# Swapping the two halves of a complex state by ScalarE copies instead of second matmuls, with the answers one pair later

## The chip, the cores and the metric

The kernel runs on one core of one Trainium2 chip. The metric is the device time of one execution in microseconds (us); the time before is the median of three runs. A profile is one further execution, taken by the hardware profiler. TensorE multiplies matrices, VectorE, ScalarE and GpSimd work on elements, and SyncE (SP) issues most DMA transfers; each engine carries out its own list of instructions in order and waits on semaphores for the others. In the profile they are PE (and PEld for weight loads), DVE, ACT, POOL and SP.

## The reference

One layer of a decoder trunk on 2048 tokens of width 1024: a norm, one input projection, three mixers side by side (A sliding window attention, B a state space model, C sparse attention), an output projection, and a feed-forward block. The change concerns mixer B, on 32 groups of 16 channels with 64 complex states each:

```python
A = lax.complex(a_re, a_im);  dt = jnp.exp(log_dt)[:, None]
A_bar = jnp.exp(A * dt)
B_bar = ((A_bar - 1.0) / A)[..., None] * Bm
Bu = jnp.einsum('blgp,gnp->blgn', uf, B_bar)
_, states = lax.associative_scan(_scan_combine, (A_bar, Bu), axis=1)   # a_r*a_l, a_r*b_l + b_r
y = jnp.einsum('blgn,gpn->blgp', states, Cm).real + D * uf
z = jax.nn.gelu(y);  ab = z @ glu_w + glu_b
out = ab[..., :W] * jax.nn.sigmoid(ab[..., W:])
```

## The kernel before

The kernel is one program in stages. The first, `phase_front` (line 81), computes the input projection in float32 by splitting each operand into a high and a low part and adding three products (`mm3`, line 74). It runs in two halves of eight row blocks. The 16 row blocks hold every 16th token each. The projection's columns come in five chunks: two u chunks (input of mixer B), then a, b and c; for each chunk `load_w` (line 128) loads eight weight slices, ScalarE converts each to its high part `wh` and VectorE computes the low part `wl`. Two buffers hold raw slices (`wr`), twelve hold `wh` and `wl`, so the last four slices of a chunk have to wait until the chunk before gives its buffers back.

In the second half the state space model is computed beside the products of the a, b and c chunks. `merge` (line 68) puts the two lists of steps together evenly: one half of a product (12 matmuls), one step of `ssm_steps` (line 430), and so on. The scheduler then orders each engine's instructions by its own estimates, so they do not stand in the order of the code. Memory for the state space model (pool `sg`, in `tp`) is that of a pool closed just before; its last user is a one-element copy on VectorE, the gate (line 201), which reads a piece of a `wl` slice. Every first use of the new memory, on whatever engine, waits for the gate.

The 32 groups go in 16 pairs (`GB = 2`). The 2048 tokens of a group lie as 128 chunks of 16. Real parts of the states lie on partitions 0 to 63, imaginary parts on 64 to 127. For pair b:

- `outer` (GpSimd): CA, the output coefficients for 17 powers of the step, three operations.
- `local` (TensorE pk, then kst on VectorE and ScalarE, then a DMA to `dkp`): the response inside a chunk.
- `turned`: `turns` (VectorE, six operations: E, rotation factors), two DMAs that make CS, which is CA with its partition halves exchanged, Wc from `dkp` by DMA, Bp (VectorE), transposes pu and pbt (TensorE), copies U and BT (ScalarE). BT holds 192 columns, the first 64 twice, so that columns 64 to 191 are the exchanged halves.
- `scanned`: pv by eight matmuls, four with the plain halves and four with the exchanged ones (line 522); m, the product with E (line 524), and the sum of its two parts; the scan Q (line 529, one instruction per group); on GpSimd St, Q times both parts of E (line 531).
- `answer`: py from four matmuls per group, two on the inputs (lines 537, 538), one on the first part of St with CA (539) and one on its second part with CS (540); then Gelu into `u_st` and `outer` of a later pair.

The steps of a pair are `scanned(b)` (with `local(b+1)` ahead of it), `turned(b+1)`, `answer(b)`. There is one St, two E, two CS.

Of the kernel before, what the change touches and what calls it, by code (L numbers as in the profile page):

```python
# [7 lines left out]
F32 = mybir.dt.float32  # L8
# [3 lines left out]
ALU = mybir.AluOpType  # L12
# [4 lines left out]
P = 128  # L17
# [63 lines left out]
def phase_front(tc, C, x, norm1_g, w_in, u_st, pd, rh_a, prm, dkp, extra):  # L81

    nc = tc.nc
    with ExitStack() as ctx:
# [96 lines left out]
        S = {}  # L181
        for half in range(2):
            box, hs = {}, []

            def steps_of(ch):
                kind, c0, n = ch
                res = [lambda: (box.update({ch: load_w(half, *ch)}), run(todo), todo.clear())]
                if ch is chunks[0]:
                    res.insert(0, lambda: hs.append(load_h(8 * half)))
                for j in range(8):  # L190
                    if ch is chunks[0] and j < 7:
                        res.append(lambda j=j: hs.append(load_h(8 * half + j + 1)))
                    for part in ((0, 1) if half and kind != "u" else (None,)):
                        res.append(lambda j=j, part=part: product(8 * half + j, hs[j], box[ch], kind, c0, n, part))
                return res
            lists = [steps_of(ch) for ch in chunks]
            with tc.tile_pool(name=f"a_x{half}", bufs=2, **({} if half else {"reuse_waits": "tile"})) as xp:
                box_x[:] = [xp]
                run(lists[0] + (lists[1] + lists[2][:1] if half else []))
                if half:  # L200
                    nc.vector.tensor_copy(xp.tile([1, 1], F32, name="gate", bufs=1), box[chunks[2]][4][1][0:1, 0:1].bitcast(F32))
            if half == 0:
                with tc.tile_pool(name="bv", bufs=1, reuse_waits="tile") as bv:
                    extra(bv, ps_t)
# [222 lines left out]
GB = 2  # L427


def ssm_steps(tc, C, S, u_st, dkp, tp, ps, ps_t):  # L430

    nc = tc.nc
    M = {}
    St = tp.tile([P, GB, 2, P], F32, name="St")
    nc.vector.memset(St[:, :, :, 0:1], 0.0)
# [7 lines left out]

    def turns(b):

        e = M["e", b] = tl([P, GB, 2, P], "E", b, 2)
        u = tl([P, 2, GB, 8, 16], "t2", f"u{b}")
        u1, u2 = u[:, 0], u[:, 1]
        ea = [S["Ea"][:, j, of(b)].unsqueeze(3).broadcast_to([P, GB, 8, 16]) for j in range(2)]
        eb = [S["Eb"][:, j, of(b)].unsqueeze(2).broadcast_to([P, GB, 8, 16]) for j in range(2)]  # L450
        o = [e[:, :, j].rearrange("p g (a b) -> p g a b", b=16) for j in range(2)]
        nc.vector.tensor_tensor(u1, ea[0], eb[0], op=ALU.mult)
        nc.vector.tensor_tensor(u2, ea[1], eb[1], op=ALU.mult)
        nc.vector.tensor_tensor(o[0], u1, u2, op=ALU.subtract)
        nc.vector.tensor_tensor(u1, ea[1], eb[0], op=ALU.mult)
        nc.vector.tensor_tensor(u2, ea[0], eb[1], op=ALU.mult)
        nc.vector.tensor_tensor(o[1], u1, u2, op=ALU.add)

    def outer(b):

        bc = [P, GB, 17, 16]
        CA, t1 = tl(bc, "CA", b, 3), tl(bc, "t1", b)
        ar, ai = (S[n][:, :, of(b)].rearrange("p t g -> p g t").unsqueeze(3).broadcast_to(bc) for n in ("AR", "AI"))
        nc.gpsimd.tensor_tensor(CA, ar, S["C1"][:, of(b)].unsqueeze(2).broadcast_to(bc), op=ALU.mult)
        nc.gpsimd.tensor_tensor(t1, ai, S["C2"][:, of(b)].unsqueeze(2).broadcast_to(bc), op=ALU.mult)
        nc.gpsimd.tensor_tensor(CA, CA, t1, op=ALU.add)
        M["c", b] = CA
# [14 lines left out]
    def turned(b):  # L482

        turns(b)
        CA = M["c", b]
        CS, Wc = tl([P, GB, 16, 16], "CS", b, 2), tl([P, GB, 256], "Wc", b, 2)
        nc.sync.dma_start(CS[0:64], CA[64:P, :, 1:17])
        nc.sync.dma_start(CS[64:P], CA[0:64, :, 1:17])
        for i in range(GB):
            base = dkp[b * GB + i]  # L490
            nc.sync.dma_start(Wc[:, i], bass.AP(base.tensor, base.offset, [[16, 8], [368, 16], [1, 256]]))
        bb = [P, GB, 16, 16]
        Bp, t2 = tl(bb, "Bp", b), tl(bb, "t2", b)
        ar, ai = (S[n][:, 0:16, of(b)].rearrange("p t g -> p g t").unsqueeze(3).broadcast_to(bb) for n in ("AR", "AI"))
        nc.vector.tensor_tensor(Bp, ar, S["Y"][:, of(b)].unsqueeze(2).broadcast_to(bb), op=ALU.mult)
        nc.vector.tensor_tensor(t2, ai, S["W"][:, of(b)].unsqueeze(2).broadcast_to(bb), op=ALU.mult)
        nc.vector.tensor_tensor(Bp, Bp, t2, op=ALU.add)
        pb = ps.tile([P, GB, 2, P], F32, tag="pb", name=f"pbt{b}", bufs=2)
        pu = ps_t.tile([P, GB, 2, P], F32, tag="pt", name=f"pu{b}")
        for i in range(GB):  # L500
            for k in range(2):
                nc.tensor.transpose(pu[:, i, k], u_st[:, b * GB + i, k * P:(k + 1) * P], C["ident"])
        U = tl([P, GB, 2, P], "U", b, 2)
        nc.scalar.copy(U, pu)
        for i in range(GB):
            for k in range(2):
                nc.tensor.transpose(pb[:, i, k], Bp[:, i, 8 * k:8 * k + 8].rearrange("p a b -> p (a b)"), C["ident"])
        BT = tl([P, GB, 2, 192], "BT", b)
        nc.scalar.copy(BT[:, :, :, 0:P], pb)
        nc.scalar.copy(BT[:, :, :, P:192], pb[:, :, :, 0:64])  # L510
        M["b", b] = BT, U, CA, CS, Wc

    def scanned(b):

        if b + 1 < NB:
            local(b + 1)
        BT, U = M["b", b][0:2]
        pv = ps.tile([P, GB, 2, P], F32, tag="pv", name=f"pv{b}")
# [1330 lines left out]
```

## Time and profile before

| | us |
|---|---|
| median of three runs | 2623.99 (2622.14 to 2625.36) |
| the profiled execution | 2620.41 |
| its span, first to last instruction | 2618.6 |

The page gives each engine's busy time over the whole span. What bounds a stage is read from the stage: busy time in a window of the span, and who waited for whom in it. An engine's idle time stands with the instruction that follows it, with the releaser behind the arrow. Matmuls overlap, so a matmul's worth is the distance from start to start, not its duration.

### The profile page before, as it was taken

The page shows a single profiled execution, that of the slowest core. Times are in us where ns is not written, and L with a number is a line of the kernel's source. Part 1 is how long each engine was busy: PE and PEld are TensorE (multiplying, and loading weights), DVE is VectorE, ACT ScalarE, POOL GpSimd, SP SyncE. Part 2 cuts the span into 40 slices and gives each one's busy share as a digit, 9 for nine tenths or more (in the row PEclk, how much of TensorE's full clock was granted, in tenths as well). Part 3 has the DMA queues.
Part 4 walks back from the last instruction along what each step waited for, and adds up shares of the span by engine and source line. Part 5 has one row for each costly group of instructions (what it writes and reads, how often), then busy time and mean ns, then how long its engine had stood idle before and what let it go on. Part 6 is the DMA issues. An engine that isn't in the chain of part 4 may idle for free. (4 is left out here: it accounts for less than half of the span.)

```text
span 2618.6 us, 38744 instructions
## 1 busy us (share of the span) xinstructions
PE 2509.6 (96%) x13096; PEld 2112.8 (81%) x13096; DVE 1784.2 (68%) x3419; ACT 1311.0 (50%) x2726; POOL 1122.8 (43%) x1179
## 2 busy tenths in 40 slices
PE   8999999899899999999989999899999999999999
PEld 7998999677677877777868888688887888888887
DVE  3835774855686667777666555755556888888886
ACT  5344332765575666655545555544444443344442
POOL 2013442221233333323266676656554445454447
PEclk9999999999999999999989999999999999999999
DMA  4342323521222111211266667665546544444435
GB/s 124 91 135 80 87 80 84 157 75 56 70 76 67 62 65 59 83 46 58 66 223 199 179 190 214 202 185 146 153 136 209 180 127 133 132 126 130 124 97 197
DMA packets 398230, 320.99 MB, mean 123 GB/s; under 512 B 52006, under 2 KB 369068, under 8 KB 396208
## 3 DMA queue, kind: packets, MB, share of 16 engines
q1 hardware_dynamic: 361936, 293.36, 37.6%
q10 hardware_dynamic: 36096, 25.17, 2.9%
q8 instruction: 103, 1.69, 0.3%
q14 instruction: 95, 0.78, 0.1%
HBM read 206.26 MB, written 107.99 MB: 120 GB/s over the span
## 5 line engine op out<-in xcount | busy, mean ns | idle before, releaser
L1335 DVE TENSOR_TENSOR v<-vr,v 128x512 fp32r<-128x512 f32 x224 | 240.0, 1080 | 76.8 <-ACT v L1334 76.4
L1334 ACT CAST v<-vr 128x512 fp32r<-128x512 f32 x224 | 139.3, 624 | 304.0 <-DMA vr<-vd 132.9
L1649 PE MATMUL pdc<-dw,v 128*128 128x512 f32 x768 | 186.4, 392 | 5.0 <-ACT dw L1334 3.2
L1649 PE MATMUL pda<-dw,v 128*128 128x512 f32 x768 | 184.5, 389 | 0.0
L1649 PE MATMUL pdb<-dw,v 128*128 128x512 f32 x768 | 184.5, 389 | 0.0
L1649 PEld LDWEIGHTS pdc<-dw,v 128*128 128x128 f32 x768 | 145.1, 189 | 36.4 <-ACT dw L1334 3.6
L1649 PEld LDWEIGHTS pda<-dw,v 128*128 128x128 f32 x768 | 144.2, 188 | 29.9
L1649 PEld LDWEIGHTS pdb<-dw,v 128*128 128x128 f32 x768 | 144.2, 188 | 29.9
L1445 POOL TENSOR_TENSOR fs<-ur,ur 128x512 f32<-128x512 f32 x64 | 96.4, 1507 | 166.2 <-DMA ur<-in_w_up 102.3
L1334 ACT CAST uh<-fs 128x512 fp32r<-128x512 f32 x128 | 78.6, 621 | 148.3 <-PE pub L1474 64.0
L1335 DVE TENSOR_TENSOR ul<-fs,uh 128x512 fp32r<-128x512 f32 x128 | 132.6, 1039 | 22.6 <-ACT uh L1334 22.3
L1335 DVE TENSOR_TENSOR ul<-ur,uh 128x512 fp32r<-128x512 f32 x96 | 101.6, 1062 | 52.4 <-ACT uh L1334 45.9
L76 PE MATMUL pw<-wo_h,mh 128*128 128x512 f32 x256 | 111.0, 434 | 4.9 <-DVE ml L1204 2.7
L857 DVE TENSOR_TENSOR tls<-pps,ths 128x512 fp32r<-128x512 f32 (+1 forms) x144 | 92.8, 658 | 29.9 <-ACT ths L856 22.3
L1490 POOL TENSOR_TENSOR ev<-e,e 128x512 f32<-128x512 f32 x64 | 96.0, 1499 | 36.4 <-ACT e L1487 26.4
L856 ACT CAST ths<-pps 128x512 fp32r<-128x512 f32 (+1 forms) x144 | 79.1, 565 | 57.0 <-PE pps L853 27.2
L77 PE MATMUL pw<-wo_l,mh 128*128 128x512 f32 x256 | 105.9, 414 | 0.0
L1474 PE MATMUL pub<-fl,uh 128*128 128x512 f32 x256 | 102.6, 401 | 3.1 <-DVE fl L1335 3.0
L78 PE MATMUL pw<-wo_h,ml 128*128 128x512 f32 x256 | 105.2, 411 | 0.0
L1474 PE MATMUL pub<-fh,uh 128*128 128x512 f32 x256 | 102.8, 402 | 1.5 <-ACT fh L1334 1.5
L1474 PE MATMUL pua<-fh,uh 128*128 128x512 f32 x256 | 101.3, 396 | 2.2 <-ACT e L1494 2.2
L1474 PE MATMUL pua<-fl,uh 128*128 128x512 f32 x256 | 101.4, 396 | 0.8 <-DVE fl L1335 0.8
(563 smaller groups left out, 7930.6 us busy)
## 6 DMA issues: line engine op xcount, KB each, us to landing
vr<-vd SPq DMA_DIRECT2D x224, 256.0 KB
ur<-in_w_up SPq DMA_DIRECT2D x128, 256.0 KB
vd<-ev SPq DMA_DIRECT2D x128, 256.0 KB
vd<-e ACTq DMA_DIRECT2D x64, 256.0 KB
dr<-in_w_down SPq DMA_DIRECT2D x32, 512.0 KB
x<-in_x SPq DMA_DIRECT2D x16, 512.0 KB
mx<-in_x SPq DMA_DIRECT2D x16, 512.0 KB
x<-mx ACTq DMA_DIRECT2D x16, 512.0 KB
```

The lines of the kernel that those rows point to most:

```text
L76: nc.tensor.matmul(out, sh, mh, start=first, stop=False)
L77: nc.tensor.matmul(out, sh, ml, start=False, stop=False)
L78: nc.tensor.matmul(out, sl, mh, start=False, stop=last)
L856: nc.scalar.copy(th[:, 0:nb], pt[:, 0:nb])
L857: nc.vector.tensor_tensor(tl[:, 0:nb], pt[:, 0:nb], th[:, 0:nb], op=ALU.subtract)
L1334: nc.scalar.copy(dh, src)
L1335: nc.vector.tensor_tensor(dl, src, dh, op=ALU.subtract)
L1445: nc.gpsimd.tensor_tensor(t, x, y, op=op)
L1474: nc.tensor.matmul(bank[b], w[:, k], h[o][:, k], start=first and k == 0 and n == 0, stop=k == HALF - 1 and n == 2, skip_group_check=True)
L1490: nc.gpsimd.tensor_tensor(tile_("v" + o), x, y, op=op)
L1649: nc.tensor.matmul(bank[b, q], x[:, q, j], y[:, j], start=first and j == 0 and n == 0, stop=j == 1 and n == 2, skip_group_check=True)
```

## The change

The exchange of the halves is made by ScalarE. `scanned` computes pv by four matmuls, copies it with its halves exchanged to vs (`swap`, two copies of 64 partitions), multiplies pv and vs each by its part of E and adds. After the scan a second `swap` makes the exchanged Q; GpSimd multiplies both by E in one instruction and subtracts one result from the other in a second. St is then a single state, and the answer needs one state matmul per group; CS with its DMAs and BT's extra columns are gone. There are two St and three E. The steps are now `scanned(b)`, `next_(b)` (`answer(b-1)`, then `local(b+1)`), `turned(b+1)` (which ends with `outer` of the pair after). The gate reads slice 3, not 4.

```diff
-                    nc.vector.tensor_copy(xp.tile([1, 1], F32, name="gate", bufs=1), box[chunks[2]][4][1][0:1, 0:1].bitcast(F32))
+                    nc.vector.tensor_copy(xp.tile([1, 1], F32, name="gate", bufs=1), box[chunks[2]][3][1][0:1, 0:1].bitcast(F32))
...
-    St = tp.tile([P, GB, 2, P], F32, name="St")
+    Ss = [tp.tile([P, GB, P], F32, name=f"St{j}", bufs=1) for j in range(2)]
...
-        e = M["e", b] = tl([P, GB, 2, P], "E", b, 2)
+        e = M["e", b] = tl([P, GB, 2, P], "E", b, 3)
...
-        nc.sync.dma_start(CS[0:64], CA[64:P, :, 1:17])
-        nc.sync.dma_start(CS[64:P], CA[0:64, :, 1:17])
...
-        BT = tl([P, GB, 2, 192], "BT", b)
-        nc.scalar.copy(BT[:, :, :, 0:P], pb)
-        nc.scalar.copy(BT[:, :, :, P:192], pb[:, :, :, 0:64])
+        BT = tl([P, GB, 2, P], "BT", b)
+        nc.scalar.copy(BT, pb)
+        M["b", b] = BT, U, CA, Wc
+        if b + 1 < NB:
+            outer(b + 1)
+
+    def swap(dst, src):
+
+        nc.scalar.copy(dst[0:64], src[64:P])
+        nc.scalar.copy(dst[64:P], src[0:64])
...
-        if b + 1 < NB:
-            local(b + 1)
...
-            for j in range(2):
-                for k in range(2):
-                    nc.tensor.matmul(pv[:, i, j], BT[:, i, k, 64 * j:64 * j + P], U[:, i, k], start=k == 0, stop=k == 1)
-        m, e = tl([P, GB, 2, P], "m", b), M.pop(("e", b))
-        nc.vector.tensor_tensor(m, pv, e, op=ALU.mult)
+            for k in range(2):
+                nc.tensor.matmul(pv[:, i], BT[:, i, k], U[:, i, k], start=k == 0, stop=k == 1)
+        m, e, vs = tl([P, GB, 2, P], "m", b), M.pop(("e", b)), tl([P, GB, P], "vs", b)
+        swap(vs, pv)
+        nc.vector.tensor_tensor(m[:, :, 0], pv, e[:, :, 0], op=ALU.mult)
+        nc.vector.tensor_tensor(m[:, :, 1], vs, e[:, :, 1], op=ALU.mult)
...
-        nc.gpsimd.tensor_tensor(St[:, :, :, 1:P], Q[:, :, 0:n].unsqueeze(2).broadcast_to([P, GB, 2, n]), e[:, :, :, 0:n], op=ALU.mult)
+        swap(Q[:, 1], Q[:, 0])
+        n, t = P - 1, tl([P, 2, GB, P], "t3", b)
+        nc.gpsimd.tensor_tensor(t[:, :, :, 0:n], Q[:, :, :, 0:n], e.rearrange("p g j c -> p j g c")[:, :, :, 0:n], op=ALU.mult)
+        nc.gpsimd.tensor_tensor(Ss[b % 2][:, :, 1:P], t[:, 0, :, 0:n], t[:, 1, :, 0:n], op=ALU.subtract)
...
-            nc.tensor.matmul(py[:, i], St[:, i, 0], CA[:, i, 1:17].rearrange("p a b -> p (a b)"), start=False, stop=False)
-            nc.tensor.matmul(py[:, i], St[:, i, 1], CS[:, i].rearrange("p a b -> p (a b)"), start=False, stop=True)
+            nc.tensor.matmul(py[:, i], Ss[b % 2][:, i], CA[:, i, 1:17].rearrange("p a b -> p (a b)"), start=False, stop=True)
...
-        if b + 2 < NB:
-            outer(b + 2)
...
+    def next_(b):
+        if b:
+            answer(b - 1)
+        if b + 1 < NB:
+            local(b + 1)
```

The order moves with it. On VectorE at the start of the state space model before (wl1_a0_4 is the low part of the fifth slice of the a chunk, t2u0, E0 and Bp0 are temporaries, rotation factors and input coefficients of pair 0):

```order
L144 SCALAR_TENSOR_TENSOR wl1_a0_3_2872<-wr1_a0_3_2869,g1_111,wh1_a0_3_2871 128x384
L144 SCALAR_TENSOR_TENSOR wl1_a0_4_2878<-wr1_a0_4_2875,g1_111,wh1_a0_4_2877 128x384
L144 SCALAR_TENSOR_TENSOR wl1_a0_5_2884<-wr1_a0_5_2881,g1_111,wh1_a0_5_2883 128x384
L201 COPY gate_2899<-wl1_a0_4_2878 1x1
...
L144 SCALAR_TENSOR_TENSOR wl1_a0_6_2890<-wr1_a0_6_2887,g1_111,wh1_a0_6_2889 128x384
L457 TENSOR_TENSOR E0_2955<-t2u0_2956 128x2x128
L144 SCALAR_TENSOR_TENSOR wl1_a0_7_2896<-wr1_a0_7_2893,g1_111,wh1_a0_7_2895 128x384
```

The same place now:

```order
L144 SCALAR_TENSOR_TENSOR wl1_a0_3_2872<-wr1_a0_3_2869,g1_111,wh1_a0_3_2871 128x384
L201 COPY gate_2899<-wl1_a0_3_2872 1x1
...
L496 TENSOR_TENSOR Bp0_2963<-Bp0_2963,t20_2964 128x512
...
L455 TENSOR_TENSOR E1_3058<-t2u1_3059 128x2x128
...
L458 TENSOR_TENSOR E1_3058<-t2u1_3059 128x2x128
L495 TENSOR_TENSOR t21_3070<-k_AI_728,k_W_723 128x512
L144 SCALAR_TENSOR_TENSOR wl1_a0_4_2878<-wr1_a0_4_2875,g1_111,wh1_a0_4_2877 128x384
L144 SCALAR_TENSOR_TENSOR wl1_a0_5_2884<-wr1_a0_5_2881,g1_111,wh1_a0_5_2883 128x384
```

Sixteen state space instructions, all of pair 0's factors and coefficients and most of pair 1's, stand now between the gate and the fifth slice; before, the gate stood behind the sixth.

On TensorE in the middle, around the answer of pair 10 (left out are the products, and the answer's second group, which repeats the first), before:

```order
L475 MATMUL pk11_4246<-CA11_4223,k_Y_722 128x256 x2
L522 MATMUL pv10_4253<-U10_4191,BT10_4197 128x128 x8
L502 MATMUL pu11_4337<-c_ident_60,u_st_83 128x128 x4
L507 MATMUL pbt11_4336<-c_ident_60,Bp11_4331 128x128 x4
...
L537 MATMUL py10_4364<-Wc10_4175,U10_4191 128x256
L538 MATMUL py10_4364<-Wc10_4175,U10_4191 128x128
L539 MATMUL py10_4364<-CA10_4107,St_2905 128x256
L540 MATMUL py10_4364<-CS10_4174,St_2905 128x256
```

and now:

```order
L476 MATMUL pk11_4244<-CA11_4180,k_Y_722 128x256 x2
L501 MATMUL pu11_4316<-c_ident_60,u_st_83 128x128 x4
L506 MATMUL pbt11_4315<-c_ident_60,Bp11_4310 128x128 x4
...
L524 MATMUL pv11_4347<-U11_4321,BT11_4327 128x128 x4
...
L543 MATMUL py10_4385<-Wc10_4158,U10_4172 128x256
L544 MATMUL py10_4385<-Wc10_4158,U10_4172 128x128
L545 MATMUL py10_4385<-CA10_4061,St0_2905 128x256
...
L476 MATMUL pk12_4393<-CA12_4329,k_Y_722 128x256 x2
```

Between the scan of pair 10 and its answer there is now the pv of pair 11; pv has four matmuls, the answer one on the state per group, and pk comes behind the answer.

On ScalarE at the same place (kst, U and BT of a pair, Gelu into u_st, po the result of a product, sq its squares), before:

```order
L479 COPY kst11_4249<-pk11_4246 16x2x240
L504 COPY U11_4342<-pu11_4337 128x512
L509 COPY BT11_4348<-pbt11_4336 128x4x128
L510 COPY BT11_4348<-pbt11_4336 128x4x64
L541 ACTIVATE u_st_83<-py10_4364 128x512
L167 ACTIVATE po8_c_4391<-pm8_c0_4351,r8_2119 128x396
```

and now:

```order
L480 COPY kst11_4247<-pk11_4244 16x2x240
L503 COPY U11_4321<-pu11_4316 128x512
L508 COPY BT11_4327<-pbt11_4315 128x512
L515 COPY vs11_4353<-pv11_4347 64x256
L516 COPY vs11_4353<-pv11_4347 64x256
L167 ACTIVATE po8_c_4379<-pm8_c0_4334,r8_2119 128x396
L169 ACTIVATE sq8_c_4381<-po8_c_4379 128x128
L515 COPY Q11_4359<-Q11_4359 64x256
L516 COPY Q11_4359<-Q11_4359 64x256
L546 ACTIVATE u_st_83<-py10_4385 128x512
L480 COPY kst12_4396<-pk12_4393 16x2x240
```

Four copies of 64 partitions stand now between BT and the Gelu, the last two behind a wait for the scan on VectorE.

## Rows read from the trace of the kernel before

**Rows 1.** Page, part 1: busy us, share of the span, instructions.

```profile
PE 2509.6 (96%) x13096; PEld 2112.8 (81%) x13096; DVE 1784.2 (68%) x3419; ACT 1311.0 (50%) x2726; POOL 1122.8 (43%) x1179
```

**Rows 2.** Busy time by stage: window, length, engines, granted clock, DMA share, GB/s.

```profile
core 0: us, PE busy (x) PEld busy (x) DVE busy (x) ACT busy (x) POOL busy (x), PEclk, DMA share, GB/s
222.00:235.00 13.00, 13.00 (x112) 13.00 (x111) 1.76 (x7) 2.90 (x6) 0.28 (x1) 1.00 0.11 33
235.00:258.00 23.00, 16.80 (x78) 15.23 (x78) 22.19 (x29) 6.65 (x13) 13.84 (x10) 0.78 0.36 92
258.00:458.00 200.00, 196.40 (x1203) 188.49 (x1202) 125.58 (x253) 65.88 (x133) 72.72 (x57) 0.99 0.31 85
```

**Rows 3.** Timeline, TensorE in the middle: start us, duration us, instruction.

```profile
301.22 0.59 PE L540 MATMUL py<-CS,St 128*128 128x256 f32 x2
...
301.65 0.60 PE L537 MATMUL py<-Wc,U 128*128 128x256 f32 x2
...
306.12 1.95 PE L522 MATMUL pv<-U,BT 128*128 128x128 f32 x16
...
307.83 0.42 PE L76 MATMUL pm_a<-wh_a,hh 128*128 128x384 f32 x1
```

**Rows 4.** Groups, 258 to 458 us: count, busy us, mean ns, idle before, releaser.

```profile
L531 POOL TENSOR_TENSOR St<-Q,E 128x508 f32<-128x508 f32 x16 | 21.4, 1335 | 79.2 <-DVE Q L529 50.4 <-DMA wr_b<-in_w_in 9.7 <-PE pm_b L78 6.6
L539 PE MATMUL py<-CA,St 128*128 128x256 f32 x64 | 19.9, 393 | 3.6 <-POOL St L531 3.6
...
L529 DVE TENSOR_TENSOR_SCAN Q<-k_rho,m 128x128 f32<-128x128 f32 x32 | 11.8, 412 | 0.5
...
L453 DVE TENSOR_TENSOR t2u<-k_Ea,k_Eb 128x256 f32<-128x256 f32 x13 | 11.8, 908 | 0.0
...
L452 DVE TENSOR_TENSOR t2u<-k_Ea,k_Eb 128x256 f32<-128x256 f32 x13 | 11.2, 865 | 0.4
...
L524 DVE TENSOR_TENSOR m<-pv,E 128x512 f32<-128x512 f32 x15 | 10.3, 688 | 13.9 <-PE pv L522 13.9
...
L495 DVE TENSOR_TENSOR Bp<-k_AR,k_Y 128x512 f32<-128x512 f32 x14 | 9.6, 684 | 0.0
...
L525 DVE TENSOR_TENSOR m<-m 128x256 f32<-128x256 f32 x16 | 6.8, 425 | 0.5
L454 DVE TENSOR_TENSOR E<-t2u 128x256 f32<-128x256 f32 x14 | 6.0, 426 | 19.0 <-POOL St L531 19.0
...
L510 ACT COPY BT<-pbt 128x256 f32<-128x256 f32 x15 | 5.9, 390 | 0.0
```

**Rows 5.** Timeline, the start: [idle before, releaser].

```profile
233.29 1.15 DVE L144 SCALAR_TENSOR_TENSOR wl_a<-wr_a,g,wh_a 128x384 fp32r<-128x384 f32 x2 [11.11 <-ACT wh_a L143]
234.36 0.13 DVE L201 COPY gate<-wl_a 1x1 f32<-1x1 f32 x1
...
234.72 1.37 POOL L464 TENSOR_TENSOR CA<-k_AR,k_C 128x544 f32<-128x544 f32 x1 [22.98 <-DVE gate L201]
...
236.45 1.12 ACT L143 ACTIVATE wh_a<-wr_a,g 128x384 fp32r<-128x384 f32 x2 [0.84 <-DVE t2u L453]
...
240.48 2.08 PE L475 MATMUL pk<-CA,k_Y 128*128 128x256 f32 x4 [3.27 <-POOL CA L466]
...
249.75 1.11 PE L507 MATMUL pbt<-c_ident,Bp 128*128 128x128 f32 x4 [2.25 <-DVE Bp L497]
...
250.52 0.67 PE L76 MATMUL pm_a<-wh_a,hh 128*128 128x384 f32 x1
```

**Rows 6.** Timeline, VectorE and GpSimd side by side.

```profile
234.97 1.39 DVE L453 TENSOR_TENSOR t2u<-k_Ea,k_Eb 128x256 f32<-128x256 f32 x1
...
247.66 1.49 POOL L465 TENSOR_TENSOR t<-k_AI,k_C 128x544 f32<-128x544 f32 x1
...
249.73 0.42 DVE L452 TENSOR_TENSOR t2u<-k_Ea,k_Eb 128x256 f32<-128x256 f32 x1
```

**Rows 7.** Groups of the whole span, GpSimd on 256 columns.

```profile
L877 POOL TENSOR_TENSOR oa<-ota 128x256 f32<-128x256 f32 x16 | 12.1, 757 | 37.7 <-ACT esa L946 8.7 <-issue 6.4 <-PE cpt L714 6.0
```

**Rows 8.** DMA issues, 258 to 458 us: queue, count, KB each.

```profile
CS<-CA SPq DMA_DIRECT2D x28, 128.0 KB
```

More of the change, by code (lines that the diff above doesn't have):

```diff
@@ L433, in ssm_steps @@
     M = {}
-    St = tp.tile([P, GB, 2, P], F32, name="St")
-    nc.vector.memset(St[:, :, :, 0:1], 0.0)
+    Ss = [tp.tile([P, GB, P], F32, name=f"St{j}", bufs=1) for j in range(2)]
+    for t in Ss:
+        nc.vector.memset(t[:, :, 0:1], 0.0)
     NB = G // GB
@@ L485, in turned @@
         CA = M["c", b]
-        CS, Wc = tl([P, GB, 16, 16], "CS", b, 2), tl([P, GB, 256], "Wc", b, 2)
-        nc.sync.dma_start(CS[0:64], CA[64:P, :, 1:17])
-        nc.sync.dma_start(CS[64:P], CA[0:64, :, 1:17])
+        Wc = tl([P, GB, 256], "Wc", b, 2)
         for i in range(GB):
@@ L507, in turned @@
                 nc.tensor.transpose(pb[:, i, k], Bp[:, i, 8 * k:8 * k + 8].rearrange("p a b -> p (a b)"), C["ident"])
-        BT = tl([P, GB, 2, 192], "BT", b)
-        nc.scalar.copy(BT[:, :, :, 0:P], pb)
-        nc.scalar.copy(BT[:, :, :, P:192], pb[:, :, :, 0:64])
-        M["b", b] = BT, U, CA, CS, Wc
+        BT = tl([P, GB, 2, P], "BT", b)
[6 more added lines that the diff above has]
+        nc.scalar.copy(dst[64:P], src[0:64])
@@ L513, in scanned @@
     def scanned(b):
-        if b + 1 < NB:
-            local(b + 1)
         BT, U = M["b", b][0:2]
-        pv = ps.tile([P, GB, 2, P], F32, tag="pv", name=f"pv{b}")
+        pv = ps.tile([P, GB, P], F32, tag="pv", name=f"pv{b}")
         for i in range(GB):
-            for j in range(2):
-                for k in range(2):
-                    nc.tensor.matmul(pv[:, i, j], BT[:, i, k, 64 * j:64 * j + P], U[:, i, k], start=k == 0, stop=k == 1)
-        m, e = tl([P, GB, 2, P], "m", b), M.pop(("e", b))
@@ L524, in scanned @@
-        nc.vector.tensor_tensor(m, pv, e, op=ALU.mult)
+            for k in range(2):
[4 more added lines that the diff above has]
+        nc.vector.tensor_tensor(m[:, :, 1], vs, e[:, :, 1], op=ALU.mult)
         nc.vector.tensor_tensor(m[:, :, 0], m[:, :, 0], m[:, :, 1], op=ALU.add)
-        Q = tl([P, GB, P], "Q", b)
+        Q = tl([P, 2, GB, P], "Q", b)
@@ L527, in scanned @@
         for i in range(GB):
             g = b * GB + i
-            nc.vector.tensor_tensor_scan(Q[:, i], S["rho16"][:, g:g + 1].to_broadcast([P, P]), m[:, i, 0], 0.0, op0=ALU.mult, op1=ALU.add)
-        n = P - 1
-        nc.gpsimd.tensor_tensor(St[:, :, :, 1:P], Q[:, :, 0:n].unsqueeze(2).broadcast_to([P, GB, 2, n]), e[:, :, :, 0:n], op=ALU.mult)
+            nc.vector.tensor_tensor_scan(Q[:, 0, i], S["rho16"][:, g:g + 1].to_broadcast([P, P]), m[:, i, 0], 0.0, op0=ALU.mult, op1=ALU.add)
+        swap(Q[:, 1], Q[:, 0])
@@ L533, in answer @@
+        n, t = P - 1, tl([P, 2, GB, P], "t3", b)
+        nc.gpsimd.tensor_tensor(t[:, :, :, 0:n], Q[:, :, :, 0:n], e.rearrange("p g j c -> p j g c")[:, :, :, 0:n], op=ALU.mult)
+        nc.gpsimd.tensor_tensor(Ss[b % 2][:, :, 1:P], t[:, 0, :, 0:n], t[:, 1, :, 0:n], op=ALU.subtract)
     def answer(b):
-        _, U, CA, CS, Wc = M.pop(("b", b))
+        _, U, CA, Wc = M.pop(("b", b))
         py = ps.tile([P, GB, 256], F32, tag="py", name=f"py{b}")
@@ L538, in answer @@
             nc.tensor.matmul(py[:, i, P:256], U[:, i, 0], Wc[:, i, 0:P], start=False, stop=False)
-            nc.tensor.matmul(py[:, i], St[:, i, 0], CA[:, i, 1:17].rearrange("p a b -> p (a b)"), start=False, stop=False)
-            nc.tensor.matmul(py[:, i], St[:, i, 1], CS[:, i].rearrange("p a b -> p (a b)"), start=False, stop=True)
+            nc.tensor.matmul(py[:, i], Ss[b % 2][:, i], CA[:, i, 1:17].rearrange("p a b -> p (a b)"), start=False, stop=True)
         nc.scalar.activation(u_st[:, of(b)], py, AF.Gelu_apprx_tanh)
-        if b + 2 < NB:
-            outer(b + 2)
     def first():
         outer(0)
-        outer(1)
         local(0)
+    def next_(b):
[3 more added lines that the diff above has]
+            local(b + 1)
     res = [first, lambda: turned(0)]
     for b in range(NB):
-        res.append(lambda b=b: scanned(b))
+        res += [lambda b=b: scanned(b), lambda b=b: next_(b)]
         if b + 1 < NB:
             res.append(lambda b=b: turned(b + 1))
-        res.append(lambda b=b: answer(b))
-    return res
+    return res + [lambda: answer(NB - 1)]
 def gelu2(nc, t, out, y):
```

## The prediction

> **What bounds the kernel now.** I read the page's busy shares first. TensorE is busy for 96% of the span, VectorE 68%, ScalarE 50%, GpSimd 43% [rows 1]; the reader should take from it only that a stage which gives TensorE less to do can pay everywhere. The stage view comes second, cut at the two ends of the stretch that the diff touches (from the second half's last u product to the end of the front). [...] So there are two places with different limits: a start in which TensorE waits for VectorE and GpSimd, and 200 us in which TensorE sets the pace. The 16 pairs of the state space model share those 200 us, 12.5 us each. Third, the timeline inside one pair, for what a removed matmul is worth [rows 3]. Fourth, the groups of instructions of the stretch, for the other engines' durations and for what TensorE waited for: only the matmul on the state waits, 3.6 us in all, for GpSimd's St [rows 4].
>
> **What goes from TensorE.** Eight pv matmuls of a pair start at 306.12 and the next matmul at 307.83, 1.71 us [rows 3]; four of eight remain, so 0.855 us go per pair, 13.7 us over 16. The second state matmul of a group holds the engine from 301.22 to 301.65, 0.43 us [rows 3]; 32 of them go, 13.8 us. Together 27.5 us, and all of it lies on the engine that sets the pace. The 3.6 us wait for St goes too, since an answer now stands a pair behind its scan; I count 2.8 of it, leaving 0.8 for the last pair, where only two half products and one answer (an estimate: some 2 us each, 6 us) stand between pv and the state matmul.
>
> **What the other engines get.** ScalarE loses one 128x256 BT copy (0.39 us) and gains four copies of 64 partitions by 256. The trace has no 64-partition copy; the nearest row is that 128x256 copy from PSUM, 0.39 us [rows 4], which I take; at twice that the balance below still holds. Per pair that is +1.17 us, 18.7 us over the stretch: 85 of about 170 us (115 at the doubled price). VectorE changes one m product of 0.688 us into two of 0.425 [rows 4]: +2.6 us in all. GpSimd gains a subtract of 128x254, nearest row 0.757 us for 128x256 [rows 7]: +12.1 us, to 84.8. The third E buffer takes away VectorE's waits for St, 19.0 us [rows 4]; those were idle time beside a busy TensorE and count nothing. On SP's queue 28 CS transfers of this stretch disappear [rows 8]; no TensorE wait is put down to them, so nothing is counted. The dkp write and the Wc read now stand close together there and hold the weight loads and the stores behind them, but Wc is needed a pair later than before: 0.
>
> **Is TensorE still last?** New waits: ScalarE now waits for pv and then for the scan, and behind the second wait stand the Gelu, the kst copy, U and BT, for which the next pv waits; VectorE waits for the vs copy, and behind it stand the scans. The chain from pv to the state is two copies 0.78, m 0.43, add 0.43, two scans 0.82, two copies 0.78, product 1.34, subtract 0.76 [rows 4, 7]: 5.3 us, 6.7 with six handoffs at 0.23, the gap from the gate's end to GpSimd's start [rows 5]. It has more than one pair, 10.6 us. That wait stays hidden in the middle.
>
> The danger is the pairing of VectorE with GpSimd. From 234.97 to 249.73 us VectorE ran 11 instructions in 14.8 us while GpSimd ran ten without a gap [rows 6]. Their undisturbed durations (five of 128x256 at 0.42, three of 128x512 at 0.69, two weight splits at 0.57, one of 0.17) make 5.5 us. So in the time that GpSimd runs, 0.63 of VectorE's time can be lost. In 258 to 458 us it lost little: the two first E products average 0.908 and 0.865 instead of 0.42 [rows 4], 12.1 us, so VectorE's work without loss is about 113.5 us, 116 after the change. If all of GpSimd's 84.8 us now cost 0.63, VectorE needs 116 + 53 = 169 us; TensorE needs 200 - 27.5 - 2.8 = 170. The two would be level, and with local bunching (16 weight splits come in two bursts, and VectorE waits once a pair for pk and for pv) TensorE would sometimes wait. I charge 5 us; bounds 0 and the rival below.
>
> [...]
>
> **The start.** The gate copy now reads the split weights of the fourth slice, not the fifth. Before, VectorE sat idle for 11.11 us ahead of the fifth and sixth (233.29), then the gate ran at 234.36 and GpSimd, idle for 22.98 us, began the first CA; TensorE waited 3.27 us for CA and 2.25 us for Bp, its clock fell in the same stretch [rows 2], and the second product began at 250.52 [rows 5]. With the gate at about 222.2, CA stands by 228 and the first pk waits for nothing. But 16 instructions of VectorE are now ahead of the fifth slice. At 1.34 us each (14.8/11) while GpSimd's ten run (14.4 us), 10.7 are done at 236.7, the rest at 239.1: the fifth slice is split 6 us later than before, and TensorE, which stood before pk at 237.2 (240.48 - 3.27) and needs about 0.9 for it, wants the split at 238. It waits 1.7 us. The seventh slice's load is issued only after that split; before, ScalarE could convert it 2.6 us after it (236.45) [rows 5], so its split ends at 243.4, the eighth's at 244, and the half product at 244.5. Transposes to 245.4, against 250.52: 5.1 us won. ScalarE has the first b conversion, which waits for its load, ahead of the first U and BT: about 0.6 back. I take 4.5. Bounds: nothing won, and all of the idle time (23.0 - 16.8 = 6.2) plus 0.22 of the busy time for the clock, 3.7: 10.
>
> **The sum.** 27.5 + 2.8 + 4.5 - 5 = 29.8 us off. The profiled execution took 2620.4 us (span 2618.6): 2590.6. The runs' median, 2624.0, is 3.6 us above it, and the new kernel is timed the same way: 2594.
>
> **The rivals.**
> 1. *The start gives all it can and VectorE keeps up*: 27.5 + 2.8 + 10 = 40.3 off, 2584. For it: VectorE and GpSimd idle from 222 to 235 us [rows 2]. Against it: the order on VectorE.
> 2. *VectorE becomes the bound.* 169 us of work, and the 13.9 us for which it waits for pv [rows 4] remain because it is in order: 183 us for the stretch, so 17 + 4.5 = 21.5 off, 2602; with waits for the swaps on top, 2612. For it: the slowed instructions [rows 6], more GpSimd work. Against it: in the steady stretch only 12 of GpSimd's 73 us cost VectorE anything.
> 3. *Slower: a ring of VectorE and ScalarE.* Each pair needs two visits to ScalarE in the middle of VectorE's chain, both queues in order. If VectorE is slowed throughout (169/16 = 10.6 us a pair), waits for both swaps (0.78 and a handoff of 0.23 each, 2.0) and for pv (13.9/16 = 0.9), a pair takes 13.5 us. It decides as soon as a pair needs more than today's 12.5. 16 x 1.0 = 16 us lost, 4.5 won: 2624 + 11.5 = 2636. Against it: between vs and the add VectorE has instructions of the next pair to fill the wait.
> 4. *The removed time is not there*: TensorE is relieved, but waits as long for BT and kst in ScalarE's queue (2 us a pair) and the start gives nothing: within 5 us of before. For it: BT stands behind kst in that queue. Against it: a half product lies between.
>
> **How the numbers follow.** Forecast 0.55, its own range 2587 to 2600; rival 1 0.14; rival 2 0.18; rival 3 0.08; rival 4 0.05. A measurement of this kernel cannot tell less than 0.2%, 5 us, from no change. Faster is the forecast with rivals 1 and 2: 0.87; same 0.05; slower 0.08. The range 2579 to 2613 takes in rivals 1 and 2 with the bounds of the start and leaves out rivals 3 and 4 and tails.
>
> **What the profile of the changed kernel would show.** Right: pv with 128 matmul records instead of 256 and no second state matmul; some 30 us less from the first pk to the end of the front, the later stages unchanged; TensorE busy for over 95% of the steady stretch; no wait of the state matmul for GpSimd but in the last pair; the gate near 222 us, no wait of pk for CA, and a wait for the fifth slice's split. VectorE's share in the stretch should rise to between 75 and 95%. Wrong: TensorE waits for Bp, BT or the split weights in the steady stretch (VectorE or ScalarE is last), a 64-partition copy over 0.8 us, or the first half product complete only near 250 us as before.

## The result, and the profile after

The changed kernel takes 2605.77 us (median of 4 runs, 2603.62 to 2609.15), the kernel before, timed beside it, 2624.68: a ratio of 0.993 with a 95% interval of 0.9913 to 0.9947, 18.9 us off. The forecast was 2594, range 2579 to 2613: the direction and the range held, the forecast's own range of 2587 to 2600 did not, and two fifths of the gain were missing. The profiled execution after took 2609.15 us (span 2607.0), the longest of its four runs, so the account is made from landmarks inside the span. The front's second half runs from the first pm_a to the first bpfs (the next stage's first matmul): before from 234.94 to 458.48 us, 223.5 us, after from 234.43 to 440.46, 206.0. That is 17.5 us less. The code of the remaining stages was not changed; in these two executions they took 6.4 us longer after (2166.6 us from the first bpfs to the end, before 2160.1), so the two spans differ by 11.6 us only. In the profiles of the runs below that length lies between 2161.2 and 2165.8 us.

The busy time by stage, to be read against [rows 2] (the last row is a part of the one above it):

```profile
core 0: us, PE busy (x) PEld busy (x) DVE busy (x) ACT busy (x) POOL busy (x), PEclk, DMA share, GB/s
222.00:235.00 13.00, 13.00 (x110) 13.00 (x110) 12.83 (x10) 3.28 (x7) 12.76 (x9) 1.00 0.10 30
235.00:258.00 23.00, 18.88 (x99) 17.47 (x98) 16.61 (x35) 10.05 (x21) 3.84 (x4) 0.85 0.31 86
258.00:440.46 182.46, 168.85 (x990) 161.09 (x989) 138.24 (x256) 79.90 (x173) 90.04 (x72) 0.97 0.25 71
300.00:320.00 20.00, 15.26 (x83) 14.21 (x82) 19.48 (x33) 11.07 (x23) 12.71 (x10) 0.91 0.41 101
```

VectorE and GpSimd now work in the 13 us in which both were idle, and the start keeps TensorE busier. But in the steady stretch TensorE is idle for 182.46 - 168.85 = 13.6 us, where it had 3.6, and its granted clock is 0.97, before 0.99. What it waited for, from 234 to 441 us (us in total, times, longest):

```profile
PE pv L524 <- ACT BT L508: 13.6, 7, 4.8
PE pm_a L77 <- DVE wl_a L144: 2.1, 1, 2.1
PE pm_a L76 <- ACT wh_a L143: 2.0, 1, 2.0
```

The wait of the state matmul for GpSimd [rows 4] is gone, and all of the steady stretch's idle time stands in one row: pv waits for BT. The groups (columns as in [rows 4]) show the new prices, 258 to 440.46 us:

```profile
L536 POOL TENSOR_TENSOR t<-Q,E 128x508 f32<-128x508 f32 x15 | 21.0, 1403 | 87.2 <-ACT Q L516 87.2
L545 PE MATMUL py<-CA,St 128*128 128x256 f32 x64 | 19.1, 380 | 0.0
L524 PE MATMUL pv<-U,BT 128*128 128x128 f32 x120 | 18.2, 299 | 13.6 <-ACT BT L508 13.6
...
L537 POOL TENSOR_TENSOR St<-t 128x254 f32<-128x254 f32 x16 | 15.2, 953 | 0.7
```

The worst of the seven waits, first VectorE and GpSimd, then ScalarE, then TensorE (start, duration, instruction, in brackets the idle time before and its releaser):

```profile
334.81 1.55 DVE L454 TENSOR_TENSOR t2u<-k_Ea,k_Eb 128x256 f32<-128x256 f32 x1
336.46 1.20 DVE L455 TENSOR_TENSOR E<-t2u 128x256 f32<-128x256 f32 x1
...
340.50 1.27 DVE L458 TENSOR_TENSOR E<-t2u 128x256 f32<-128x256 f32 x1
341.70 0.41 DVE L527 TENSOR_TENSOR m<-pv,E 128x256 f32<-128x256 f32 x1
...
343.42 0.74 DVE L533 TENSOR_TENSOR_SCAN Q<-k_rho,m 128x128 f32<-128x128 f32 x2
...
334.57 1.51 POOL L467 TENSOR_TENSOR CA<-CA,t 128x544 f32<-128x544 f32 x1
...
340.26 1.24 POOL L466 TENSOR_TENSOR t<-k_AI,k_C 128x544 f32<-128x544 f32 x1
...
334.89 0.37 ACT L516 COPY vs<-pv 64x256 f32<-64x256 f32 x1
...
344.24 0.40 ACT L515 COPY Q<-Q 64x256 f32<-64x256 f32 x1 [6.96 <-DVE kst L479]
344.66 0.40 ACT L516 COPY Q<-Q 64x256 f32<-64x256 f32 x1
345.09 0.55 ACT L480 COPY kst<-pk 16x480 f32<-16x480 f32 x1
...
346.80 0.56 ACT L508 COPY BT<-pbt 128x512 f32<-128x512 f32 x1
...
339.87 0.60 PE L506 MATMUL pbt<-c_ident,Bp 128*128 128x128 f32 x4
...
347.41 2.08 PE L524 MATMUL pv<-U,BT 128*128 128x128 f32 x8 [4.85 <-ACT BT L508]
```

Read it backwards. pv waits for BT. TensorE had transposed BT's input by 340.5; the copy is late because it stands behind the Q swap in ScalarE's queue, and the Q swap waited 6.96 us for the scan. (The row names kst's addition, 0.15 us that stand right behind the scans on VectorE; in all twelve waits of the Q swap, whichever of the two the row names, the swap began 0.09 us after the scan's end.) The scan was late because VectorE has the next pair's six E instructions ahead of m, for which vs lay ready at 335.3, and while GpSimd ran its outer product five of them took 1.2 to 1.6 us each (0.42 when alone, as at 249.73 us in [rows 6]). Once GpSimd is done, the products are back at 0.41. In two of the seven waits (319.63 and 382.62 us) it is another instruction of ScalarE that waits, kst's copy:

```profile
318.07 0.55 ACT L480 COPY kst<-pk 16x480 f32<-16x480 f32 x1 [1.77 <-DVE kst L479]
318.53 0.57 ACT L503 COPY U<-pu 128x512 f32<-128x512 f32 x1
319.01 0.57 ACT L508 COPY BT<-pbt 128x512 f32<-128x512 f32 x1
```

### The profile page after: what moved, and what is told of

The parts are those of the page before. It is cut to its first block, busy times and chain, and to the rows that moved or that the text cites. A ratio compares the mean times of both kernels' runs of the same rounds, so it can differ in the third digit from the quotient of the medians.

```text
span 2607.0 us, 38424 instructions
## 1 busy us (share of the span) xinstructions
PE 2487.8 (95%) x12904; PEld 2089.8 (80%) x12904; DVE 1802.0 (69%) x3436; ACT 1328.8 (51%) x2774; POOL 1141.6 (44%) x1195
## 5 line engine op out<-in xcount | busy, mean ns | idle before, releaser
L863 ACT CAST ths<-pps 128x512 fp32r<-128x512 f32 (+1 forms) x144 | 79.1, 565 | 57.4 <-PE pps L860 27.5
L1481 PE MATMUL puc<-fl,uh 128*128 128x512 f32 x256 | 101.3, 396 | 4.8 <-DVE fl L1342 4.8
L1481 PE MATMUL puc<-fh,uh 128*128 128x512 f32 x256 | 101.5, 397 | 3.9 <-ACT fh L1341 2.5
```

Of the source, the lines that this page charges most:

```text
L863: nc.scalar.copy(th[:, 0:nb], pt[:, 0:nb])
L1481: nc.tensor.matmul(bank[b], w[:, k], h[o][:, k], start=first and k == 0 and n == 0, stop=k == HALF - 1 and n == 2, skip_group_check=True)
```

## The experiments

"Front" is the length from first pm_a to first bpfs in each kernel's profile; the ratio is to the kernel before on the same chip, with its 95% interval. The first theory: VectorE, slowed by GpSimd, makes the scan late, and the Q swap in ScalarE's queue hands the lateness to BT. Rivals: the start lost the gain; ScalarE's queue is enough by itself; VectorE has too much work whatever GpSimd does.

**The gate, alone and undone.** On the kernel before: `box[chunks[2]][4]` becomes `[3]` in the gate copy.

> The kernel before with one edit alone: the gate copy reads the split weights of the fourth slice, not the fifth. Theory: in the changed kernel the start was worth 3.5 us (second product at 246.98, before 250.52), and that comes from this edit, so here too the second product begins at 246 to 248 us and the time falls by 3 to 5 us against the kernel before. Rival (the start is where the forecast gain was lost): second product at 249 to 251 us, time within 1.5 us of before.

2621.21 us, 0.9996 (0.9987 to 1.0005). The second product begins at 246.17 us, as the theory had it, and the time is within the rival's 1.5 us. The front is 218.3 us, 5.3 shorter, and pk waits for nothing, but the time shows at most 3.4 us of it: in this one profile the next stage, to the first pub, is 4.2 us longer than before. On the changed kernel, the reverse edit:

> The changed kernel with the gate copy reading the split weights of the fifth slice again, as before. The gate edit alone moved the kernel before by 1.4 us (0.9996, 0.9987 to 1.0005), though its front was 5.3 us shorter. Theory: the start of the changed kernel goes back to waits for CA and Bp, the second product begins 3 to 4 us later after the first, the front is 3 to 6 us longer and the time 0 to 5 us more than the changed kernel's. Rival (the gate matters more here, where GpSimd has more to do): 6 us or more.

2610.02 us, 0.9945 (0.993 to 0.996); front 212.9 us, 6.8 longer, with 3.3 us waits for CA and for Bp as in [rows 5]. From first pm_a to the second product it is 15.6 us with the old gate in both kernels and 12.6 with the new one, so the start itself is worth 3.0 us, against 4.5 forecast. The whole front differs by more, 5.3 and 6.8 us (in the second case over the 3 to 6 expected), and what reaches the end is not settled better than 0 to 5 us.

**GpSimd's load cut.** In outer():

```
-        nc.gpsimd.tensor_tensor(t1, ai, S["C2"]..., op=ALU.mult)
-        nc.gpsimd.tensor_tensor(CA, CA, t1, op=ALU.add)
```

> The changed kernel with GpSimd's outer product cut to its first multiplication; the second multiplication and the addition are left out, so the values are others. ScalarE's queue is as in the changed kernel. Theory (BT is late because the Q swap ahead of it waits for a scan that is late through VectorE's slowed two-SBUF instructions): TensorE's 13.6 us of waits for BT fall below 3, the E products L453 to L458 of the turned pairs come back to 0.42 to 0.6 us each, the front's stretch from the first pm_a to the first bpfs falls from 206.0 to 190 to 195 us. Rival 1 (ScalarE's queue order alone makes BT late): the waits for BT stay at 10 to 14 us, the stretch at 203 to 206. Rival 3 (VectorE has too much work even undisturbed): VectorE stays above 85% of the stretch and TensorE goes on waiting for it.

2579.77 us, 0.9837 (0.9818 to 0.9857); front 182.5 us, below what was expected.

```profile
232.72:258.00 25.28, 25.28 (x155) 24.49 (x154) 17.86 (x40) 13.84 (x28) 3.37 (x3) 1.00 0.38 110
258.00:415.24 157.24, 154.62 (x938) 148.17 (x937) 103.91 (x241) 76.95 (x167) 49.23 (x46) 1.00 0.26 77
```

From 222 us to the end of the front ScalarE, VectorE and TensorE carry out the changed kernel's instructions in the changed kernel's order, and TensorE waits for BT only 2.6 us: the queue alone is no cause. The start has no gap at all and the clock is 1.00 throughout. VectorE is busy for 36 us less with nearly the same instructions (131.6 us from 222 us on, in the changed kernel 167.7).

**The Q swap taken out of BT's way, two ways.** First the Q swap and the state behind the next pair's BT, then the Q swap by VectorE:

```
+        one = tl([P, 1], "one", b, 2)        # in turned(b), behind the BT copy: 1.0, made from BT
+        nc.scalar.activation(one, BT[:, 0, 0, 0:1], AF.Copy, scale=0.0, bias=1.0)
+        state(b - 1, one)                    # the two Q copies with scale=one, then t and St
```
```
-        swap(Q[:, 1], Q[:, 0])
+        nc.vector.tensor_copy(Q[0:64, 1], Q[64:P, 0])
+        nc.vector.tensor_copy(Q[64:P, 1], Q[0:64, 0])
```

> The changed kernel with the Q swap and the state placed on ScalarE behind the BT copy of the next pair (a one-column tile made from BT scales the Q copies by 1 and so holds them there; values unchanged). VectorE and GpSimd do the same work as in the changed kernel, and GpSimd goes on slowing VectorE. Theory: ScalarE's queue carries the lateness to BT, so TensorE's waits for BT fall from 13.6 to below 3 us, the stretch from first pm_a to first bpfs from 206.0 to 189 to 194 us, the time by 12 to 16 us against the changed kernel, to about 2591. Rival (VectorE is the bound, the queue only shows it): TensorE's waits move to Bp, the transposes or the state, and the stretch stays at 202 to 207 us. Second rival: the state comes too late for the answer, and TensorE waits for GpSimd's St instead, 5 to 15 us.

> The changed kernel with the Q swap as two VectorE copies behind the scans, not ScalarE copies: ScalarE then never waits for a scan, and VectorE has 32 copies of 64 partitions by 256 more, some 13 us at 0.4 us each. Theory (ScalarE's wait for the scan is what holds BT): waits for BT below 4 us, and the stretch at 190 to 197 us in spite of VectorE's extra work, the time 8 to 15 us below the changed kernel. Rival (VectorE is the bound): the stretch grows by about those 13 us to 215 to 220, and TensorE waits for Bp or BT more than 13.6 us.

The theory missed in both. Behind BT: 2606.11 us, 0.9936 (0.9922 to 0.9951), front 204.6. On VectorE: 2607.74, 0.9944 (0.9929 to 0.9959), front 210.1, waits for BT 15.3 us. The first front lies in the range of its rival (202 to 207), but the waits stayed at BT; the second lies between theory and rival. In the first the waits fell by 4 us only, and ScalarE waited elsewhere (30.8 us for the same addition in the second):

```profile
PE pv L529 <- ACT BT L508: 9.5, 5, 2.9
PE py L555 <- POOL St L547: 2.3, 4, 0.7
...
ACT kst L480 <- DVE kst L479: 38.6, 14, 5.3
```

**Do the two engines' times add?** After these three runs the theory was a plain sum of VectorE and GpSimd, an assumption of mine. The tests: the state on VectorE (`nc.gpsimd` becomes `nc.vector` in the t product and the subtraction); Ea in PSUM, where the products of the turns then have one PSUM input; both; and the pv half of the change alone.

> The changed kernel with the state's product and subtraction on VectorE, not GpSimd (values unchanged). New theory after the runs with a shorter outer product and with BT first: VectorE and GpSimd exclude each other in instructions with two SBUF inputs, so their times add; between 258 us and the end of the front the changed kernel has 108 us of VectorE work without loss and 90 of GpSimd, 14 of it not exposed, 184 in 182.5 us. Here VectorE has 17.8 us more (0.69 and 0.42 a pair), GpSimd 37.7 less (1.40 and 0.95 a pair): 164, about TensorE's own. The waits for BT fall below 5 us, the stretch from first pm_a to first bpfs from 206.0 to 185 to 193, the time by 12 to 20 us against the changed kernel. Rival (VectorE simply has too much work, whatever GpSimd does): 17.8 us more on it make the stretch 210 to 222 us and the kernel slower than the changed one.

2601.97 us, 0.9915 (0.9898 to 0.9931), front 203.8. Faster by 4 us, not by 12 to 20, with intervals that overlap, and the front is not longer: both sides were wrong. GpSimd lost 37 us of work, yet TensorE still waited 10.8 us, in three waits for BT, and ScalarE 25.5 us for the scan and 24.0 for kst.

```
+    bank = ps.tile([P, 4, P], F32, name="bank", bufs=1)      # pv in columns 0:2, Ep in 2:4
+            nc.scalar.copy(Ep, S["Ea"][:, :, b * GB:b * GB + G // 2])   # at pairs 0 and 8
-        ea = [S["Ea"][:, j, of(b)]...]
+        ea = [Ep[:, j, h * GB:h * GB + GB]...]
```

> The changed kernel with the table Ea copied by ScalarE, half of it at a time, into the free half of pv's PSUM bank and read from there, so that the four products of the turns (L453, L454, L456, L457 in the changed kernel) have one PSUM and one SBUF input; nothing else moves, values unchanged. Theory (exclusion of two-SBUF instructions): these four come back to 0.42 to 0.46 us each, 27 us of VectorE's work leave the sum, 184 becomes 157, and the stretch falls from 206.0 to 184 to 194, the time by 10 to 20 us. Rival a (the products are slow for their broadcast inputs or for lack of issue, not for SBUF): they stay at 0.5 to 0.96 us and nothing changes. Rival b (GpSimd takes its toll of whatever VectorE runs beside it): the four come back but others grow as much, the stretch stays at 200 to 206.

> Both edits together: the state on VectorE and Ea in PSUM. Theory: the sum of the two engines is 137 us, well under TensorE's, so TensorE sets the pace: waits for BT below 3 us, the stretch 180 to 187 us (182.5 with the shorter outer product), the time about 2580. Rival (VectorE's own work is the bound): VectorE above 90% of the stretch, which stays at 195 or more.

Slower than the changed kernel: 2616.3 us, 0.9968 (0.9955 to 0.9981), front 218.4; and with both edits 2625.21, 0.9999 (0.9989 to 1.0008), front 223.9. The groups of the first, 258 to 430 us:

```profile
L501 DVE TENSOR_TENSOR Bp<-Bp,t 128x512 f32<-128x512 f32 x13 | 17.5, 1344 | 0.2
L500 DVE TENSOR_TENSOR t<-k_AI,k_W 128x512 f32<-128x512 f32 x13 | 16.4, 1264 | 0.3
L463 DVE TENSOR_TENSOR E<-t2u 128x256 f32<-128x256 f32 x13 | 15.6, 1196 | 0.3
...
L461 DVE TENSOR_TENSOR t2u<-bank,k_Eb 128x256 f32<-128x256 f32 x13 | 5.5, 421 | 0.2
L459 DVE TENSOR_TENSOR t2u<-bank,k_Eb 128x256 f32<-128x256 f32 x13 | 5.4, 417 | 0.0
```

The four products are at 0.42 us, as expected, and three of their neighbours with two SBUF inputs at 1.2 to 1.3. But it was not one edit: as Ea shares a tile with pv, the turns now stand behind the m products in VectorE's order and Bp comes last, and TensorE waited 24.9 us for Bp, 32.2 with both edits. So it says nothing on what the slowing of the two-SBUF instructions is worth.

> The pv half of the change alone: the halves of pv exchanged by ScalarE, the later answers and the gate as in the changed kernel, but the state product by GpSimd on both halves with a second state matmul and the CS copies by DMA, as before; no Q swap, no subtraction. (m and vs are written in place, for space.) TensorE has 13.8 us more than in the changed kernel, GpSimd about 15 less. Theory: 108 + 75 - 14 = 169 us for the two engines, so TensorE, 170 + 13.8 = 184, sets the pace again and waits for BT below 4 us; the stretch is 203 to 209 us, level with the whole change: the state half of the change gave TensorE 13.8 us and took them back through GpSimd. Rival (the subtraction costs nothing, and the loss in the changed kernel is ScalarE's queue or VectorE's own work): the stretch is longer by the 13.8 us, 216 to 222.

2612.78 us, 0.9955 (0.994 to 0.997), front 212.0: between the two expectations. TensorE is 12.6 us busier than in the changed kernel, and idle 6.6 less (11.1 of 212.0, against 17.7 of 206.0). So the state half gives back, as idle time of TensorE, half of what it takes off; a sum of engine times did not tell how much.

**Two waits, not one.** In the run with BT first, the wait that remained ahead of BT is kst's. Its two parts are read from partitions 0 to 15 of one PSUM tile, pk, by VectorE and then ScalarE, and the second reader waits for the first (38.6 us above). With the reads in the other order, in the two runs below, it was VectorE that waited for ScalarE: 20.7 us in ten waits with that order alone, and 2.9 us in one wait with the Q swap behind BT. So in both orders the second reader waited, and which comes second is free to choose. This wait is not new. In the kernel before, over 258 to 458.48 us, it was

```profile
ACT kst L479 <- DVE kst L478: 24.1, 11, 3.3
```

and TensorE waited for BT not once. Turned round:

```
+        nc.scalar.copy(kst[:, :, 16:256], pk[0:16, :, 16:256])
         nc.vector.tensor_tensor(kst[:, :, 0:16], pk[0:16, :, 0:16], S["dD"][:, of(b)], op=ALU.add)
-        nc.scalar.copy(kst[:, :, 16:256], pk[0:16, :, 16:256])
```

> The changed kernel with this edit alone: kst's ScalarE copy ahead of its VectorE addition; the Q swap stands where the changed kernel has it. Theory: one of ScalarE's two waits for VectorE ahead of BT is left, so TensorE's waits for BT stay at 7 to 13 us and the stretch at 201 to 206. Rival (kst's addition is the only wait that matters): waits below 4 us, the stretch below 195.

> The kernel with the Q swap behind BT, and kst's ScalarE copy issued ahead of kst's VectorE addition (both read pk's PSUM tile, and whichever is issued second waits for the other). With the Q swap behind BT alone, TensorE still waited 9.5 us for BT, and ScalarE 38.6 us for kst's addition, which stands ahead of U and BT in its queue. VectorE and GpSimd do the same work, values unchanged. Theory (VectorE is late through GpSimd, and reaches TensorE through what ScalarE waits for ahead of BT, two waits and not one): TensorE's waits for BT fall from 9.5 to below 3 us, the granted clock stays near 1.00, and the stretch from first pm_a to first bpfs falls from 204.6 to 186 to 194; the time to 2587 to 2595. Rival (VectorE beside GpSimd is the bound itself): the waits move to Bp, pv or St, and the stretch stays above 200.

Alone: 2609.06 us, 0.994 (0.9925 to 0.9955), front 205.9; ScalarE's wait for kst became a longer wait for the scan, and the waits for BT stayed, a little above the range expected:

```profile
ACT Q L515 <- DVE Q L533: 47.8, 11, 10.8
PE pv L524 <- ACT BT L508: 14.0, 8, 5.0
```

With the Q swap behind BT: 2595.67 us, 0.9891 (0.9877 to 0.9906), front 197.7, 10 us below the changed kernel with intervals that do not meet. TensorE's wait in the steady stretch, then VectorE's groups and the stage:

```profile
PE py L555 <- POOL St L547: 6.4, 4, 3.5
```
```profile
L538 DVE TENSOR_TENSOR_SCAN Q<-k_rho,m 128x128 f32<-128x128 f32 x30 | 19.8, 700 | 0.3
L495 DVE TENSOR_TENSOR t<-k_AI,k_W 128x512 f32<-128x512 f32 x13 | 14.6, 1124 | 0.0
```
```profile
258.00:430.09 172.09, 165.69 (x979) 158.56 (x979) 134.63 (x254) 87.38 (x188) 88.94 (x73) 0.98 0.25 74
```

No wait for BT is left, with VectorE nearly as slow as before (134.6 us busy against 138.2; the scans now take part of the slowing, 0.70 us against 0.41) and GpSimd's 89 us unchanged. Either edit alone gave nothing. The front stayed 4 us above the range expected, and TensorE waits 6.4 us for St. Its two long waits, at 307.31 and 331.79 us, lie where VectorE is busy for 37.4 of 40 us (300 to 340), so the rival's move of the waits to St holds in part; whether the later place of the state or VectorE makes them was not tested.

**The addition in outer() on VectorE, on top of that** (`nc.gpsimd` becomes `nc.vector` in the third line).

> As the kernel with the Q swap behind BT and kst's copy first, and the addition in the outer product on VectorE, not GpSimd (values unchanged): GpSimd has 16 x 1.6 = 25 us less, VectorE 16 x 0.73 = 12 more. If GpSimd's time beside VectorE still costs something once ScalarE's queue is free of VectorE, the stretch is 3 to 8 us shorter than without this edit. Rival (TensorE sets the pace by then): level within 2 us. Second rival (VectorE's work is the bound): 5 us or more longer.

2592.98 us, 0.988 (0.9863 to 0.9898), front 194.3: the fastest that leaves nothing out. Its front is 3.4 us shorter, at the low end of the 3 to 8 expected; the intervals of the two times overlap.

## Why the prediction was right in direction and short in size

- **TensorE's 27.5 us: right.** Busy time times granted clock, by the two rows of each front (pieces at 235 and 258 us, cut to the landmarks): before 16.86 x 0.78 + 196.88 x 0.99 = 208.1, after 19.45 x 0.86 + 168.85 x 0.97 = 180.5. 27.6 us of full-speed work went, within about 1 us for the rounded clock. The run with the lean outer product, at a clock of 1.00, has 179.9.
- **The wait for St, 2.8: right**, all 3.6 went.
- **The start, 4.5: too high by a third.** CA came in time and pk waited for nothing. TensorE waited 2.15 us for the fifth slice's split, at 239.88 (forecast 1.7, at 239.1), and 1.97 more for the seventh slice's conversion; the second product began at 246.98 (forecast 245.4, before 250.52). Idle time in the start fell by 2.1 us and the clock's loss by 1.0 (0.22 x 16.86 against 0.14 x 19.45): 3.1, as the two runs of the gate have it (3.0).
- **The 5 us for VectorE beside GpSimd: the step that failed.** The waits for BT are 13.6 us, and the clock lost 0.03 x 168.9 = 5.1 us of the steady stretch, before 0.01 x 196.9 = 2.0: 16.7 in all. 27.6 + 3.6 + 3.1 - 16.7 = 17.6, the 17.5 us measured; this must add up but for rounding, since busy, idle and lost clock make the whole length, so it says where the time went and not why. Two things were missing in the 5 us. I charged VectorE's slowing as a matter of throughput ("the two would be level"), but VectorE, at 138 of 182 us, was not full over the stretch: what counted was that two instructions of ScalarE wait for VectorE ahead of BT. The "local bunching" of the prediction is there too. From 300 to 320 us, with six weight splits, VectorE was busy for 19.5 of 20 us, and two of the seven waits, 4.7 us, lie there. And the granted clock was lower around some of TensorE's waits: it was 0.91, 0.92 and 0.91 in the three stretches of 20 us from 300 to 360 us, with waits of 2.85, 1.89, 0.73 and 4.85 us, and 1.00 from 380 to 400 us, with one of 2.21. The eight pv matmuls took 2.08 us behind the wait of 4.85, 1.85 behind that of 1.89, and 1.16 behind those of 2.85 and 2.21 (1.05 at 360.10 us, behind none), so the length of a wait alone does not tell what it costs.
- **Rival 4 named the place** (BT behind kst in ScalarE's queue) and dismissed it with "a half product lies between". ScalarE's four waits for the scan of 5.9 to 7.4 us were longer than that hides: each was followed by a wait for BT, of 0.5, 0.7, 4.8 and 0.6 us, while six of 2.5 to 4.0 us were followed by none. Rival 3's two visits to ScalarE were the way, too, though not at its price. Rival 2 (2602 to 2612) had the better time for the wrong reason: VectorE did not become the bound of the whole stretch, since 10 us came back with its work nearly unchanged. What rival 1 promised (40 us) is in the run with the lean outer product, 41 us off the front, but only with GpSimd relieved.
- **Prices:** the 64-partition copies took 0.37 us from PSUM and 0.40 from SBUF (forecast 0.39); the product on pv stayed at 0.417; the subtraction took 0.953, not 0.757. ScalarE's load at the doubled price is 110 us by the prediction's own terms (65.9 + 16 x 2.73), not 115; nothing hung on it, as ScalarE was busy for 80. The test "TensorE over 95% of the steady stretch" failed at 92.5%, and the sign of being wrong that was named, TensorE waiting for BT there, is what came; VectorE's share, 76%, was just inside its 75 to 95%.

**What is shown and what is open.** Shown: with GpSimd's outer product cut the loss goes, and with both of ScalarE's waits taken out of BT's way (the Q swap moved behind BT, kst's copy put ahead of the addition) the waits for BT go while VectorE stays slow; either wait alone keeps them. Open: what makes the 6.4 us of waits for St that stand there instead, how the slowing is shared out (which VectorE instructions it met differed with the order: a scan took 0.41 us in the changed kernel and 0.70 with both waits out of BT's way, and a sum of the two engines failed as a rule), and why 5.3 us of the front in the run with the gate alone did not reach the end. No run shows that VectorE and GpSimd exclude each other, the term behind the sums of 184, 164, 157, 137 and 169 us. Shown in its place: in the changed kernel five E products with two SBUF inputs took 1.2 to 1.6 us each beside GpSimd's outer product, and 0.42 is what one takes alone; two products with one PSUM input took 0.42 beside its t product; and the fronts of the four runs were 203.8, 218.4, 223.9 and 212.0 us, not 185 to 193, 184 to 194, 180 to 187 and 203 to 209 (in the second and third the order on VectorE moved as well).

## What to carry to other kernels

When work moves to an engine with time to spare, list what that engine's queue will wait for and what stands behind each wait: ScalarE was 44% busy here, and still held TensorE, since its copies waited for VectorE ahead of the one copy that TensorE needed. Two waits in one queue may have to be moved together: here an edit that removed one gave nothing and seemed to refute the cause. A wait that was harmless before, as kst's was, can count after a change. Price a wait of TensorE above its length when the granted clock in the rows around it falls, as here to 0.91 around the wait of 4.85 us, behind which eight pv matmuls took 2.08 us and not 1.05.

## What the runs showed of the hardware

- The scan was slowed beside GpSimd as the products were (1.2 to 1.6 us, 0.42 alone): between 258 and 430 us it took 0.41 us on average in the changed kernel, where GpSimd was idle behind it, and 0.88, 0.70 and 0.59 in the three kernels with the Q swap behind BT (in the order of their runs). In the kernel with Ea in PSUM one pair of scans took 2.85 us, from 339.51 us on, beside two instructions of GpSimd's outer product.
- VectorE's products with one PSUM input did not slow here: beside GpSimd's t product, which ran from 343.35 to 344.73 us in the kernel with Ea in PSUM, two of them took 0.42 us each, and the addition of two SBUF tiles just ahead, beside the outer product, 0.90:

```profile
342.71 0.90 DVE L460 TENSOR_TENSOR E<-t2u 128x256 f32<-128x256 f32 x1
...
343.65 0.42 DVE L461 TENSOR_TENSOR t2u<-bank,k_Eb 128x256 f32<-128x256 f32 x1
343.99 0.42 DVE L462 TENSOR_TENSOR t2u<-bank,k_Eb 128x256 f32<-128x256 f32 x1
...
343.35 1.38 POOL L541 TENSOR_TENSOR t<-Q,E 128x508 f32<-128x508 f32 x1
```
